# The last down projection as seven block products instead of eight

## The chip, the cores and the metric

The kernel runs on one core of one Trainium2 chip. The metric is device microseconds from start to end of one execution; of a set of runs the median is given. The core's engines, as the profile calls them, are PE (TensorE: matmuls), PEld (its loading of the stationary operand), DVE (VectorE), ACT (ScalarE), POOL (GpSimd) and SP (SyncE, which here only issues DMAs).

## The reference

A decoder trunk of two layers on x of 512 positions by 1024 channels, all in float32. Each layer adds a token mixer (three branches, merged by gates, then `w_out`) and a gated MLP with a causal convolution; a last RMSNorm ends it. The change is in the MLP of the second layer and the norm behind it, and uses idle time in the stages before.

```python
D_MODEL, SEQ, DEPTH, D_FF, CONV_WIDTH = 1024, 512, 2, 2816, 3

def conv_ffn(h, w_up, conv_w, conv_b, w_down):
    S = h.shape[1]
    u = h @ w_up
    up = jnp.pad(u, ((0, 0), (CONV_WIDTH - 1, 0), (0, 0)))
    c = conv_b
    for j in range(CONV_WIDTH):
        c = c + conv_w[j] * up[:, j:j + S]
    gate, val = jnp.split(c, 2, axis=-1)
    return (jax.nn.silu(gate) * val) @ w_down

for l in range(DEPTH):
    ...
    x = x + jnp.sum(gates * proj, axis=2) @ w_out[l]
    x = x + conv_ffn(rmsnorm(x, norm2_g[l]), ffn_w_up[l], ffn_conv_w[l], ffn_conv_b[l], ffn_w_down[l])
return rmsnorm(x, final_g)
```

## The kernel before

All work of the core is written in Python loops that are fully unrolled. A framework then sets the order on each engine: it plays the program through on an estimated timeline, starts on each engine the ready instruction that stands earliest in the program (or was given high priority), hands out buffers as they come free, and adds the semaphores. An engine carries out its instructions in the order so planned. `keep_in_program_order` and `self.pin` fix the order of chosen instructions, here all matmuls of the last stage.

**Matmuls in three parts.** A float32 product is made of three matmuls on parts in the type fp32r: an operand is split into a high part (a cast by ScalarE, L135 for weights) and a low part (a subtraction by VectorE, L136), and `mm3` (matmul at L152) adds high x low, high x high and low x high into one PSUM bank. Every matmul has a stationary operand of 128x128 and a moving one of 128x512.

**Weights.** A unit is 256 KB, 128x512 float32. `unit` asks for the next one; `load` issues its DMA on SP's queue into one of `NRAW` = 3 raw buffers (tile `wr`, L122), `part` splits it. The list of units is known from a first pass, so that loads and splits run ahead of their use, by as many units as `AHEAD` allows for the pool of the unit. The pool says where the parts go: `None` to tiles `wh`, `wl` (three each); "r", "f" and "u" to tiles `sh`, `sl` in those pools; "p" to `wh`, `wl` for three units of five and to `u` tiles for the other two.

**Pools.** 31 tiles `u`, 16 tiles `r` and 39 tiles `f`, each 128x512 float32; PSUM has four banks `acc` and four banks `sm`.

**The stages around the change**, in order: layer 0 ends with `wout` (eight output tiles, 24 matmuls each), `ffn_up` and `ffn_down` (eight output tiles, 66 matmuls each, the result's tile stored to DRAM by POOL's queue). Layer 1 ends with `wout`, `ffn_up` and `last`. `ffn_up` runs over 22 rows of channels i; each has two products of 24 matmuls (gate and value), the scaling (L1054), the convolution (L1056 to L1058), the gate (L1062 to L1064) and the split of the result into `act` (L1066, L1067), two tiles of 128 channels x 512 positions. In layer 1 it also turns x into position-major tiles `xt` by way of DRAM on POOL's queue (L226, L230).

**`last`.** Here the activations are the stationary operand, 128 positions (a chunk c) at a time, and the weights move, so the result has positions on the partitions. It goes through the 1024 output columns in two halves of 512. For each half, for each of the 22 rows k: one unit of weights, four chunks c, three matmuls each. After the first half VectorE adds x piece by piece (L1106), ScalarE squares and sums, POOL multiplies by the norm's weights (L1123). In the second half the last `KEPT` = 6 units stay in `u` tiles, and the four chunks go through them one after another; each chunk's sum, square root (L1137), scaling and store follow at once. The last chunk's store ends the kernel.

Of the kernel before, what the change touches and what calls it, by code (L numbers as in the profile page):

```python
# [8 lines left out]
F32 = mybir.dt.float32  # L9
F32R = mybir.dt.float32r  # L10
# [5 lines left out]
L = 2  # L16
# [8 lines left out]
KEPT = 6  # L25
SEQ = "0 H 0 S 0 U S U S 0 S 0 0 S 2 2 Y 0 0 2 1 2 1 2 1 2 1 2 1 2 1 1 1"
# [22 lines left out]
class Emit:  # L49
# [68 lines left out]
    def load(self, u):  # L118
        name, l, i, c0, n, _ = u
        raw = self.wp.tile([128, 512], F32, name=self.nm("wr"), tag="wr", bufs=NRAW)  # L120
        with self.tc.high_priority():
            self.kept(self.nc.sync.dma_start(raw[:, :n], self.a[name][l, i][:, c0:c0 + n]))  # L122
        self.raws.append(raw)
        self.nraw += 1
# [107 lines left out]

    def norm_new(self):
        return {"z": [], "acc": None}
# [66 lines left out]
    def run(self):  # L301
        nc, tc, a, V = self.nc, self.tc, self.a, self.nc.vector
        self.con = self.cp.tile([128, NCC], F32, name="con")
        self.rst = self.cp.tile([128, 512], F32, name="rst")
# [714 lines left out]
    def wout(self, l, mg, xd, st):  # L1019
        nc, V = self.nc, self.nc.vector  # L1020
        out = []
        for m in range(8):
# [7 lines left out]
            self.norm_sq(st, xi)  # L1030
        return out


    def ffn_up(self, l, st, x):
# [4 lines left out]
        def at():  # L1039
            nt[0] += 1  # L1040
            return (self.f if nt[0] <= NFP else self.r)(dt=F32R, n="ah")
# [3 lines left out]
        for i in range(NFF):  # L1045
# [19 lines left out]
            hi, lo = at(), at()  # L1065
            A.copy(hi, th)  # L1066
            V.tensor_tensor(lo, th, hi, op=SUB)  # L1067
            act.append((hi, lo))
        return act

    def ffn_down(self, l, act, x, st):
# [3 lines left out]
        for m in range(8):  # L1075
# [7 lines left out]
            xd.append(d)  # L1083
        return x, xd


    def last(self, act):


        nc, V, A, P, po = self.nc, self.nc.vector, self.nc.scalar, self.nc.gpsimd, self.tc.keep_in_program_order  # L1090
        fg = [self.u(n="fg") for _ in range(2)]
        for h in range(2):
            nc.sync.dma_start(fg[h], self.a["fgr"][:, 512 * h:512 * h + 512].to_broadcast([128, 512]))
        ss, bias = self.small((128, NC), "fss", 1), self.small((128, NC), "fbi", 1)
        self.pin = True

        def prod(ps, k, c, w):
            cs = slice(128 * c, 128 * c + 128)
            ah, al = act[k]
            self.mm3(ps, (ah[:, cs], al[:, cs]), w, k == 0, k == NFF - 1)  # L1100

        def add(y, ps, j, c):

            b = slice(j % 4 * 128, j % 4 * 128 + 128)
            q = lambda t: t[:, b].rearrange("p (a d) -> p a d", d=32)
            return V.scalar_tensor_tensor(q(y), q(ps), 0.5, self.xt[j][:, c], op0=MUL, op1=ADD)  # L1106

        def square(y, s):
            return A.activation(self.u(n="sq")[:, 0:y.shape[1]], y, AF.Square, accum_out=s)

        self.pool = None
        pss = [self.acc() for _ in range(NC)]
        for k in range(NFF):
            w = self.unit("wdt", 0, k, 0)
            for c in range(NC):
                prod(pss[c], k, c, w)
        ya = []
        for c in range(NC):
            y = self.u(n="ya")
            for j in range(4):  # L1120
                add(y, pss[c], j, c)
            square(y, ss[:, c:c + 1])
            P.tensor_tensor(y, y, fg[0], op=MUL)  # L1123
            ya.append(y)
        V.tensor_scalar(bias, ss, 1.0 / D, 1e-6, op0=MUL, op1=ADD)
        pss = [self.sm() for _ in range(NC)]
        for k in range(NFF - KEPT):
            w = self.unit("wdt", 0, k, 512)
            for c in range(NC):
                prod(pss[c], k, c, w)  # L1130
        self.pool = "u"
        ws = [self.unit("wdt", 0, k, 512) for k in range(NFF - KEPT, NFF)]

# [7 lines left out]
        for c in range(NC - 1):  # L1141
            for k, w in enumerate(ws, NFF - KEPT):
                prod(pss[c], k, c, w)
            y, s = self.u(n="yb"), self.small((128, 1), "fs1")
            for j in range(4, 8):
                po(add(y, pss[c], j, c))
            po(square(y, s))
            rs = factor(s, bias[:, c:c + 1])
            po(A.activation(ya[c], ya[c], AF.Copy, scale=rs))
            nc.scalar.dma_start(self.a["out"][c, :, 0:512], ya[c])  # L1150
            po(V.scalar_tensor_tensor(y, y, rs, fg[1], op0=MUL, op1=MUL))
            nc.sync.dma_start(self.a["out"][c, :, 512:1024], y)
        c, y, b = NC - 1, self.u(n="yb"), bias[:, NC - 1:]
        for k, w in enumerate(ws, NFF - KEPT):
            prod(pss[c], k, c, w)
        for j in range(4, 8):
            po(add(y, pss[c], j, c))
        s = [self.small((128, 1), f"fs{i}", 1) for i in (2, 3)]
        for i in range(2):
            po(square(y[:, 256 * i:256 * i + 256], s[i]))  # L1160
        po(V.scalar_tensor_tensor(b, s[0], 1.0 / D, b, op0=MUL, op1=ADD))
        rs = factor(s[1], b)
        for i in range(2):
            h = slice(256 * i, 256 * i + 256)
            po(V.scalar_tensor_tensor(y[:, h], y[:, h], rs, fg[1][:, h], op0=MUL, op1=MUL))
# [117 lines left out]
```

## Time and profile before

| | |
|---|---|
| time, median of 3 runs | 1713.9 us (1712.93 to 1714.75) |
| span of the profiled execution, first to last instruction | 1712.1 us |
| time of the runs' median around that span | 1.8 us |
| mean granted TensorE clock of the profiled execution | 1.000 |
| `last`: first matmul, end of the last matmul | 1585.80 us, 1705.64 us |
| instructions | 27377 |

The profile is of one execution, and its own time is the span. Times in it are microseconds from its start. A line of the groups has line, engine, operation, output<-inputs, shapes and count, then busy time in all and the mean of one in ns, then the idle time of the engine before it and what ended that. In a timeline a line has start, length, engine, line and operation; what stands in brackets is the idle time before it and the releaser.

### The profile page before, as it was taken

How to read it: one execution, taken by the hardware profiler on the slowest of the kernel's cores; microseconds unless marked ns; L12 is line 12 of the kernel's file. 1: busy time of each engine (PE TensorE's matmuls, PEld its weight loads, DVE VectorE, ACT ScalarE, POOL GpSimd, SP SyncE). 2: the span in 40 equal slices, each digit the busy share in tenths (PEclk: the TensorE clock that was granted, in tenths of full speed). 3: DMA queues.
4: the chain of work that ended last, by engine and by line, in shares of the span. 5: the costliest groups of instructions: out<-in, count | busy, mean ns of one | idle time of the engine just before them, and what ended most of it. 6: DMA issues, size and time to landing. Idle time of an engine off the chain costs nothing.

```text
span 1712.1 us, 27377 instructions
## 1 busy us (share of the span) xinstructions
PE 1701.0 (99%) x10280; PEld 1392.4 (81%) x10280; DVE 1155.0 (67%) x1998; ACT 774.9 (45%) x1315; POOL 178.2 (10%) x213
## 2 busy tenths in 40 slices
PE   9999999999999999999999999999999999999998
PEld 7888777788888888888888888777888888888886
DVE  6887745578669777753368887555776787787333
ACT  6563443554255444433355634345533554444223
POOL 2121000003200000000021210100141011100010
PEclk9999999999999999999999999999999999999999
DMA  5236553525542333233432365535254433333333
GB/s 180 87 109 205 174 174 99 178 89 163 163 148 93 98 99 96 69 113 114 123 105 87 107 222 168 159 122 178 77 185 147 137 122 117 113 109 99 99 99 105
DMA packets 132325, 219.61 MB, mean 128 GB/s; under 512 B 16864, under 2 KB 37088, under 8 KB 132192
## 3 DMA queue, kind: packets, MB, share of 16 engines
q1 hardware_dynamic: 116336, 180.94, 34.4%
q0 software_dynamic: 6784, 20.98, 3.8%
q10 hardware_dynamic: 9072, 15.94, 2.6%
q8 instruction: 81, 1.33, 0.3%
q14 instruction: 52, 0.43, 0.1%
HBM read 188.43 MB, written 29.36 MB: 127 GB/s over the span
## 4 chain that ended last, share of the span: by engine, by line
PE 89%; DMA 5%; DVE 3%; ACT 1%; issue 1%; SPq 1%; ACTq 0%; POOL 0%; DVEq 0%; POOLq 0%
PE acc L152 80%; PE sm L152 4%; PE sm L640 2%; DMA wr<-wall 2%; PE sm L893 1%; DVE wl L136 1%; PE sm L547 1%; DMA ws<-sgw 1%; DMA tr<-yt 0%; DMA tr<-bkT 0%; SPq L226 0%; DMA bkS<-tr 0%; PE sm L998 0%; DMA x<-xT 0%; DMA tr<-qkt 0%
## 5 line engine op out<-in xcount | busy, mean ns | idle before, releaser
L152 PE MATMUL acc<-hi,sh 128*128 128x512 f32 x1108 | 431.9, 390 | 0.0
L152 PE MATMUL acc<-lo,sh 128*128 128x512 f32 x1108 | 431.6, 390 | 0.0
L152 PE MATMUL acc<-hi,sl 128*128 128x512 f32 x1108 | 430.6, 390 | 0.0
L135 ACT CAST sh<-wr 128x512 fp32r<-128x512 f32 (+1 forms) x347 | 212.2, 615 | 356.6 <-PE acc L152 264.3
L136 DVE TENSOR_TENSOR sl<-wr,sh 128x512 fp32r<-128x512 f32 (+1 forms) x347 | 236.1, 683 | 139.9 <-ACT sh L135 74.9
L136 DVE TENSOR_TENSOR wl<-wr,wh 128x512 fp32r<-128x512 f32 x233 | 165.2, 710 | 184.9 <-ACT wh L135 182.3
L135 ACT CAST wh<-wr 128x512 fp32r<-128x512 f32 x233 | 144.1, 619 | 281.1 <-PE acc L152 182.3
L152 PEld LDWEIGHTS acc<-hi,sl 128*128 128x128 f32 x1108 | 208.0, 188 | 43.7 <-DVE gth L1013 0.3
L152 PEld LDWEIGHTS acc<-lo,sh 128*128 128x128 f32 x1108 | 208.0, 188 | 43.6 <-issue 0.9
L152 PEld LDWEIGHTS acc<-hi,sh 128*128 128x128 f32 x1108 | 208.0, 188 | 43.6 <-issue 0.3
L152 PE MATMUL acc<-lo,wh 128*128 128x512 f32 x588 | 232.5, 395 | 0.5 <-DVE lo L211 0.3
L152 PE MATMUL acc<-hi,wl 128*128 128x512 f32 x588 | 230.3, 392 | 0.5 <-DVE wl L136 0.5
L152 PE MATMUL acc<-hi,wh 128*128 128x512 f32 x588 | 229.5, 390 | 0.0
L152 PEld LDWEIGHTS acc<-lo,wh 128*128 128x128 f32 x588 | 110.5, 188 | 26.3 <-DVE lo L211 1.6
L152 PEld LDWEIGHTS acc<-hi,wl 128*128 128x128 f32 x588 | 110.5, 188 | 25.9 <-DVE wl L136 2.3
L152 PEld LDWEIGHTS acc<-hi,wh 128*128 128x128 f32 x588 | 110.6, 188 | 22.4 <-issue 0.2
L152 PE MATMUL acc<-ah,sh 128*128 128x512 f32 x352 | 108.4, 389 | 0.0
L1054 DVE TENSOR_TENSOR fu<-acc,rsF 128x512 f32<-128x512 f32 x88 | 60.6, 688 | 56.4 <-PE acc L152 56.3
L1056 ACT ACTIVATE cv<-fu,pc 128x512 f32<-128x512 f32 x88 | 71.6, 816 | 46.7 <-DVE fu L1054 44.4
L1057 DVE SCALAR_TENSOR_TENSOR cv<-fu,pc,cv 128x511 f32<-128x511 f32 x88 | 65.8, 748 | 21.1 <-ACT cv L1056 20.6
L152 PE MATMUL acc<-wl,hi 128*128 128x512 f32 x192 | 78.3, 408 | 0.0
L152 PEld LDWEIGHTS acc<-ah,sh 128*128 128x128 f32 x352 | 66.1, 188 | 13.7
(312 smaller groups left out, 2345.4 us busy)
## 6 DMA issues: line engine op xcount, KB each, us to landing
wr<-wall SPq DMA_DIRECT2D x488, 256.0 KB, 2.7
gd<-gth ACTq DMA_DIRECT2D x48, 256.0 KB, 3.0
gth<-gd POOLq DMA_DIRECT2D x48, 256.0 KB, 3.6
wr<-wdt SPq DMA_DIRECT2D x44, 256.0 KB, 2.6
wr<-wdn SPq DMA_DIRECT2D x40, 256.0 KB, 2.7
tr<-bkT SPq DMA_DIRECT2D x16, 256.0 KB, 2.8
bkS<-tr SPq DMA_DIRECT2D x128, 32.0 KB, 2.5
tr<-vT SPq DMA_DIRECT2D x8, 256.0 KB, 2.6
```

The lines of the kernel that those rows point to most:

```text
L135: self.kept(self.nc.scalar.copy(hi[:, :n], raw[:, :n]))
L136: self.kept(self.nc.vector.tensor_tensor(lo[:, :n], raw[:, :n], hi[:, :n], op=SUB))
L152: i = self.nc.tensor.matmul(*x, **y)
L547: i = T.matmul(pK[hv[1 - h], j, :], bk[hv[h], c, 1, :], x[hv[h], c, :], start=True, stop=True)
L640: po(T.matmul(o, l, r, start=start, stop=True, skip_group_check=True))
L893: po(T.matmul(X[h][:, i, :], lhsT, rhs, start=new[h], stop=stop, skip_group_check=True))
L1054: V.tensor_tensor(u, ps, self.rsF, op=MUL)
L1056: A.activation(t, u, AF.Identity, scale=self.p("cw2", j), bias=self.p("cb", j))
L1057: V.scalar_tensor_tensor(t[:, 1:], u[:, :511], self.p("cw1", j), t[:, 1:], op0=MUL, op1=ADD)
```

## The change

Rows k are taken in 11 pairs q, positions in two halves of 256, output columns in two halves of 512. With A the activations (positions x channels) in 2x2 blocks and W the weights in 2x2 blocks, the eight block products of `last` become seven, in Winograd's form: seven products of sums of blocks, from which the four output blocks are put together. Each product runs over 11 pairs and two chunks of 128 positions, one unit of weights for each pair.

- **Sums of weights** (`presum`, new): for each pair q, at the end of an output tile's work in `wout` of layer 0 (m = 2, 5), `ffn_down` of layer 0 (m = 0 to 6) and `wout` of layer 1 (m = 2, 5), POOL's queue loads the four blocks into `u` tiles; at the next tile VectorE makes four sums of 128x512 and POOL's queue stores them to DRAM (`tsum`). `last` loads them for four of the seven products and the plain weights for three.
- **Sums of activations** (`halves`, new): in `ffn_up` of layer 1, after each odd row, five VectorE operations of 128x256 make the sums; two of the tiles are split into `act` at once, and two halves `ab` and a half `s4` go to DRAM by POOL's queue. The number of `act` tiles stays the same. `s` and `d` use the tags `wh` and `wl`.
- **`last`** first runs four products side by side (7, 5, 6, 4), over all pairs, in all eight PSUM banks, and meanwhile loads `ab` and `s4` by POOL's queue and splits them into `f` tiles. Then product 1, then 2, then 3, whose last six units stay in `u` tiles and are used by one chunk after the other. VectorE puts the outputs together meanwhile; the second half of the positions is finished and stored during product 2. The weights go to pool "p" instead of `None`. POOL's multiplications are gone.

The diff, cut to its core:

```diff
+PRE = {(0, "o", 2): 0, (0, "o", 5): 1, (0, "d", 0): 2, ..., (0, "d", 6): 8, (1, "o", 2): 9, (1, "o", 5): 10}
     def load(self, u):
+        src = self.tsum[i] if name == "tsum" else self.a[name][l, i]
+    def presum(self, l, stage, m):
+        if self.pre:
+            q, b = self.pre.pop()
+            V.tensor_tensor(b[3], b[3], b[1], op=SUB)
+            V.tensor_tensor(b[1], b[1], b[0], op=SUB)
+            V.tensor_tensor(b[0], b[0], b[3], op=ADD)
+            V.tensor_tensor(b[2], b[2], b[0], op=SUB)
+            for p, t in zip((7, 5, 6, 4), (b[3], b[1], b[0], b[2])):
+                self.tsum[q, p] = self.dp.tile([128, 512], F32, name=self.nm("ts"))
+                self.nc.gpsimd.dma_start(self.tsum[q, p], t)
+        q = PRE.get((l, stage, m))
+        if q is not None:
+            b = [self.u(n="pre") for _ in range(4)]
+            for i, t in enumerate(b):
+                self.nc.gpsimd.dma_start(t, self.a["wdt"][0, 2 * q + i // 2][:, i % 2 * 512:i % 2 * 512 + 512])
+            self.pre.append((q, b))
     def ffn_up(self, l, st, x):
...
-            act.append((hi, lo))
+            if l < L - 1:
+                act.append(self.split(th, at))
+            elif i % 2 == 0:
+                even = th
+            else:
+                act.append(self.halves(even, th, i // 2, at))
+    def halves(self, a, b, q, at):
+        s, d = [self.wp.tile([128, 512], F32, name=self.nm(t), tag=t, bufs=3) for t in ("wh", "wl")]
...
+        P.dma_start(ab[:, h[0]], a[:, h[0]])
+        P.dma_start(ab[:, h[1]], b[:, h[0]])
+        V.tensor_tensor(s[:, h[0]], a[:, h[1]], b[:, h[1]], op=ADD)
+        V.tensor_tensor(s[:, h[1]], s[:, h[0]], a[:, h[0]], op=SUB)
+        V.tensor_tensor(d[:, h[0]], b[:, h[0]], s[:, h[1]], op=SUB)
+        P.dma_start(self.s4[:, h[q % 2]], d[:, h[0]])
+        V.tensor_tensor(b[:, h[0]], a[:, h[0]], a[:, h[1]], op=SUB)
+        return self.split(s, at), self.split(b, at), ab, self.s4
     def last(self, act):
...
+        pss = {p: [(self.acc if p in (7, 5) else self.sm)() for _ in range(2)] for p in (7, 5, 6, 4)}
+        self.pool, ab, s4 = "p", [], []
+        for q in range(Q):
+            s, t = act[q][:2]
+            for p in (7, 5, 6, 4) if q < Q - 1 else (6, 7, 5, 4):
+                w = unit(p, q)
+                x, at = {7: (t, 0), 5: (s, 0), 6: (s, 256), 4: (t, 256)}[p]
+                for r in range(2):
+                    prod(pss[p][r], x, at, r, w, q == 0, q == Q - 1)
...
+            nc.gpsimd.dma_start(o, act[q][2])
+            ab.append(self.split(o, self.f))
...
+        for q in range(3):
+            w = unit(1, q)
+            for r in range(2):
+                go(1, q, r, w)
+        (e: ACT copies of product 6; f, g: combinations of 7, 5, 4 with it, eight in all)
+        for q in range(3, Q):
+            w = unit(1, q)
...
+            if q < 6:
+                for r in range(2):
+                    addx((v1, v2, v3)[q - 3][r], int(q > 3), r + 2 * (q < 5))
+        (product 2, first three pairs; product 1 added to v1, v2, v3 and, with x, to v0;
+         product 2, other pairs, with the norm and the stores of chunks 2 and 3)
+        for q in range(Q - KEPT):
+            w = unit(3, q)
...
+        self.pool = "u"
+        ws = [unit(3, q) for q in range(Q - KEPT, Q)]
+        for r in range(2):
+            for q, w in enumerate(ws, Q - KEPT):
+                go(3, q, r, w)
+            y, ya, b = v3[r], v0[r], ss[:, r:r + 1]
+            po(plus(y, out[3][r], y))
...
```

More of the change, by code (lines that the diff above doesn't have):

```diff
@@ L1102, in add, with unit, prod @@
[L1102 to L1106, printed above, removed]
+        def unit(p, q):
+            if p > 3:
+                return self.unit("tsum", 0, (q, p), 0)
+            return self.unit("wdt", 0, 2 * q + (p > 1), 512 * (p == 3))
+        def prod(ps, x, at, r, w, first, end):
+            cs = slice(at + 128 * r, at + 128 * r + 128)
+            self.mm3(ps, (x[0][:, cs], x[1][:, cs]), w, first, end)
@@ L1139, in factor @@
             return rs
[L1141 to L1152, printed above, removed]
@@ new lines, in last @@
+        out[3] = [self.acc() for _ in range(2)]
+        for q in range(Q - KEPT):
+            w = unit(3, q)
+            for r in range(2):
+                go(3, q, r, w)
+            if q == 1:
+                for r in range(2):
+                    b = ss[:, r:r + 1]
+                    plus(v0[r], out[2][r], v0[r])
+                    square(v0[r], b)
+                    V.tensor_scalar(b, b, 1.0 / D, 1e-6, op0=MUL, op1=ADD)
+                    V.tensor_tensor(v0[r], v0[r], fg[0], op=MUL)
```

157 lines of the change are left out of this document (107 added, 50 removed).

## The prediction

> **What bounds the kernel now.** I read the page first, then the busy time by stage, then the engines' timelines inside the last stage.
>
> ```profile
> span 1712.1 us, 27377 instructions
> PE 1701.0 (99%) x10280; PEld 1392.4 (81%) x10280; DVE 1155.0 (67%) x1998; ACT 774.9 (45%) x1315; POOL 178.2 (10%) x213
> PE 89%; DMA 5%; DVE 3%; ACT 1%; issue 1%; SPq 1%; ACTq 0%; POOL 0%; DVEq 0%; POOLq 0%
> ```
>
> TensorE is busy 99% of the span and carries 89% of the chain that ended last. The stage view (core 0; columns: length, busy and count of PE, PEld, DVE, ACT, POOL, clock, DMA share, GB/s) says the same of each stage that the change touches: ffn_down of layer 0, ffn_up of layer 1, and `last`.
>
> ```profile
> 700.00:800.00 100.00, 100.00 (x443) 82.81 (x442) 54.14 (x88) 36.10 (x61) 1.62 (x3) 1.00 0.33 97
> 1400.00:1500.00 100.00, 100.00 (x443) 82.78 (x442) 78.44 (x121) 45.72 (x72) 10.93 (x20) 1.00 0.37 114
> 1580.00:1645.00 65.00, 65.00 (x288) 53.64 (x287) 23.44 (x38) 17.57 (x28) 0.00 (x0) 1.00 0.31 101
> 1645.00:1679.00 34.00, 34.00 (x152) 28.15 (x151) 13.42 (x27) 10.47 (x21) 5.95 (x4) 1.00 0.33 100
> ```
>
> In `last` nothing but matmuls counts: PE never idles and VectorE is a third busy. What a matmul costs there is not its printed duration. The timeline of PE at the start of `last` and at its end:
>
> ```profile
> 1585.80 0.39 PE L152 MATMUL acc<-wl,ah 128*128 128x512 f32 x1
> 1586.48 0.39 PE L152 MATMUL acc<-wl,ah 128*128 128x512 f32 x1
> 1587.16 0.39 PE L152 MATMUL acc<-wl,ah 128*128 128x512 f32 x1
> 1705.03 0.61 PE L152 MATMUL sm<-sh,ah 128*128 128x512 f32 x2
> ```
>
> Each line opens a triple of three matmuls. Triples start 0.68 us apart, so a matmul takes 0.2267 us although each is shown as 0.39: they overlap. The stage has 22 rows x 2 halves x 4 chunks x 3 = 528 matmuls; 528 x 0.2267 = 119.7 us, and from 1585.80 to the end at 1705.64 it is 119.84. The tail after it is 6.5 us.
>
> **What the change removes.** Seven products x 11 pairs x 2 chunks x 3 = 462 matmuls: 66 fewer, 66 x 0.2267 = 15.0 us. (At the printed 0.39 us it would be 25.7; the pitch decides.) If PE stayed full, `last` would take 104.7 us.
>
> **What it asks in return: weights.** Before, one weight unit (256 KB load, cast by ScalarE, subtraction by VectorE) serves 12 matmuls, 2.72 us. Now a unit serves 6, 1.36 us, and there are 77 units instead of 44. No steady stage of before asks for more than one unit in 2.72 us, so the rate must come from a burst. There is one: near the end the last loads go to tiles that are free, and nothing but the three raw buffers (`NRAW`) holds them back. ScalarE's casts, then some of VectorE's subtractions, then SyncE's issues:
>
> ```profile
> 1679.72 0.62 ACT L135 CAST sh<-wr 128x512 fp32r<-128x512 f32 x1 [0.62 <-DMA wr<-wdt]
> 1681.20 0.62 ACT L135 CAST wh<-wr 128x512 fp32r<-128x512 f32 x1 [0.86 <-PE sm L152]
> 1682.50 0.62 ACT L135 CAST sh<-wr 128x512 fp32r<-128x512 f32 x1 [0.68 <-DMA wr<-wdt]
> 1684.08 0.62 ACT L135 CAST sh<-wr 128x512 fp32r<-128x512 f32 x1 [0.95 <-DMA wr<-wdt]
> 1685.43 0.62 ACT L135 CAST sh<-wr 128x512 fp32r<-128x512 f32 x1 [0.74 <-DMA wr<-wdt]
> 1686.94 0.62 ACT L135 CAST sh<-wr 128x512 fp32r<-128x512 f32 x1 [0.88 <-DMA wr<-wdt]
> 1688.41 0.62 ACT L135 CAST sh<-wr 128x512 fp32r<-128x512 f32 x1 [0.85 <-DMA wr<-wdt]
> ...
> 1680.37 0.69 DVE L136 TENSOR_TENSOR sl<-wr,sh 128x512 fp32r<-128x512 f32 x1 [0.55 <-ACT sh L135]
> 1684.73 0.69 DVE L136 TENSOR_TENSOR sl<-wr,sh 128x512 fp32r<-128x512 f32 x1 [0.88 <-ACT sh L135]
> ...
> 1681.09 0.33 SPq L122 DMA_DIRECT2D wr<-wdt  x1
> 1685.45 0.33 SPq L122 DMA_DIRECT2D wr<-wdt  x1
> ```
>
> Six intervals from 1679.72 to 1688.41 give 1.45 us a unit. One buffer's round: its subtraction ends at 1680.37 + 0.69 = 1681.06, SyncE issues at 1681.09, the next weights land and are cast at 1684.08 (3.02 us after the release), the subtraction ends at 1684.73 + 0.69 = 1685.42, and SyncE issues again at 1685.45. The round is 4.36 us; three buffers give 1.45 us. That is more than the 1.36 that PE now asks for, with VectorE and ScalarE otherwise idle and no other transfers. So in the new stage the supply of weights, not PE, ends last.
>
> **What is in stock at the start.** While ffn_up ends, weights of `last` are loaded ahead:
>
> ```profile
> 1583.36 0.33 SPq L122 DMA_DIRECT2D wr<-wdt  x1
> 1590.22 0.33 SPq L122 DMA_DIRECT2D wr<-wdt  x1
> 1580.84 0.69 DVE L136 TENSOR_TENSOR wl<-wr,wh 128x512 fp32r<-128x512 f32 x1 [0.18 <-ACT wh L135]
> ```
>
> By 1583.4 six loads were out, three split and three waiting for a `wh` tile; SyncE then stood until PE gave one back. In the new stage every five units take three `wh`/`wl` tiles and two `u` pairs, so five units can be split and three more landed when PE starts. Unit 5 is split once unit 0 is used (1.36 + 0.65 + 0.69 = 2.7 us), its buffer loads unit 8, which is ready 3.0 + 1.34 later, at 7.0 us; PE wants it at 8 x 1.36 = 10.9. With c the us per unit, the 77th unit is ready at 7.0 + 68c, and after it PE still has 3 + 18 matmuls (the six kept units go through chunk 0, then chunk 1): 4.8 us. So the stage takes 11.8 + 68c, never less than 104.7. Against 119.7 the gain is 107.9 - 68c: 9.3 us at c = 1.45, 5.2 at 1.51, nothing at 1.587, and the full 15.0 only below 1.367.
>
> **What raises c.** Other transfers: 11 `ab` and 6 `s4` loads of 256 KB on POOL's queue during the first 44 units. Landing (last column, us) beside such loads in the merges, in a stretch with more traffic (175 GB/s), in the present `last` and in its burst:
>
> ```profile
> wr<-wall SPq DMA_DIRECT2D x49, 256.0 KB, 2.8
> gth<-gd POOLq DMA_DIRECT2D x22, 256.0 KB, 3.6
> ...
> wr<-wall SPq DMA_DIRECT2D x37, 256.0 KB, 3.2
> ...
> wr<-wdt SPq DMA_DIRECT2D x27, 256.0 KB, 2.6
> ...
> wr<-wdt SPq DMA_DIRECT2D x5, 256.0 KB, 2.9
> ```
>
> The new stage moves 256 KB per 1.45 us, 181 GB/s, plus about 40 for `ab` and `s4`. From the burst's 2.9 to 3.2 is +0.3 on a round, +0.1 on c, at most for the loads that meet another; I take +0.03. The Trainium skill, DMA: Bandwidth & Descriptors, section Latency and other measured facts, puts HBM access at 0.2 us on average and 2 us under high load; that speaks against any change that nearly doubles a stage's loads. If the whole 1.8 us came on top, c would be (4.36 + 1.8)/3 = 2.05, an estimate from that page; the rows above show tenths so far.
>
> VectorE and ScalarE: behind each unit's split stand the new operations. Prices by the nearest rows (mean ns of one after the comma):
>
> ```profile
> L1054 DVE TENSOR_TENSOR fu<-acc,rsF 128x512 f32<-128x512 f32 x3 | 2.1, 687 | 1.2 <-PE acc L152 1.2
> L1106 DVE SCALAR_TENSOR_TENSOR ya<-acc,xt 128x128 f32<-128x128 f32 x16 | 3.4, 280 | 2.1 <-PE acc L152 2.1
> 1644.61 2.26 DVE L1106 SCALAR_TENSOR_TENSOR ya<-acc,xt 128x128 f32<-128x128 f32 x11
> L1165 DVE SCALAR_TENSOR_TENSOR yb<-yb,frs,fg 128x256 f32<-128x256 f32 x2 | 0.9, 481 | 0.0
> L1151 DVE SCALAR_TENSOR_TENSOR yb<-yb,frs,fg 128x512 f32<-128x512 f32 x3 | 2.3, 752 | 0.1
> L1137 ACT ACT_TABLE_LOAD x1 | 1.3, 1283 | 0.0
> ```
>
> In the first 44 units: one more split per four units and half of one. A split of 0.6 us fits into the 1.45 us round behind the unit's own; half of them collide for some 0.3 us: +0.04 on c. In products 1 and 2 (22 units, 32 us at 1.45) VectorE has 22 x 0.65 = 14 us of splits, 14 combinations of a full tile x 0.69 = 9.7, 32 pieces of 128x128 at 2.26/11 = 0.205 = 6.6, and four scalings x 0.75 = 3: 33 us. It is full, so a split often finds an operation in front of it: half of 0.69 at every second round, +0.06 to +0.1, and part spills into the last product, which has little else. The square root's table load (1.3 us) moves here from the first chunk of the end, beside a stock of nothing; once. Together c = 1.51. Bounds: the round with the shortest landing of the burst, released at 1679.82 and cast at 1682.50, is 2.68 + 1.34 = 4.02, c = 1.34 (full gain); one 0.69 us operation ahead of every split gives (4.36 + 0.69)/3 = 1.68 (6.3 us lost).
>
> **The rest.** Sums of weights: 11 steps x 4 VectorE operations x 0.69 us = 30 us, and 88 transfers of 256 KB on POOL's queue. ffn_down of layer 0, where seven of the steps lie, has VectorE 54% busy and PE at 100% beside it; free. In w_out a step's 2 MB meet weights that PE wants one per 2.72 us, with three raw buffers and three split units in hand (8 us): I take 0.5 us in all, 0 to 3. What queues behind these on POOL is the store of x for the next layer, long before its use. ffn_up of layer 1: five half-width operations per pair, by the row above 0.48 each, 2.4 us in the 96 matmuls x 0.2267 = 21.8 of a pair; VectorE's 78% becomes 89%; PE has four accumulators, and covers it. Without that cover it would be 2.4 us once, at the last pair. Three stores per pair on POOL: hidden. Tail: one full-tile operation instead of four quarter ones (0.69 against 0.89): 0.2 won; otherwise the same.
>
> Sum: 107.9 - 68 x 1.51 = 5.2, + 0.2, - 0.5 = 4.9 won. The profiled span would be 1707.2. The runs' median of 1713.9 lies 1.8 above the span, so 1709.0.
>
> **Rivals.** (a) *VectorE takes the gain*: with every split behind one whole operation, products 1 and 2 and the `ab` splits alike, c = 1.68 and the stage is 6.3 us longer: 1720.2 less the tail's 0.2, plus 0.5: 1720.5. It decides from 1.587 on, that is 0.4 us of added wait in a round of 4.36. For it: 33 us of work in 32. Against: splits are given high priority when the order is planned, and the other operations have until the next product. (b) *PE stays the bound*: c below 1.367, 15 us won: 1698.9. Only the shortest landing speaks for it. (c) *Landings grow with load*: by the longest landing seen for such a load, about 1.1 us over the burst's (4.0 against 2.9), as in the answer on the weight buffer:
>
> ```profile
> DMA to landing us min/median/max: 2.4/2.6/4.0
> ```
>
> c = (4.36 + 1.1)/3 = 1.82 and 15.9 us lost: 1730. (The Trainium skill's rule named above would be worse still.) Against: it is the longest, and the median is 2.6. (d) *The two cancel*: c from 1.54 to 1.63, within 3.4 us of now.
>
> **How the numbers follow.** 0.2% is 3.4 us, about what a measurement of this kernel can tell from no change. Forecast, c from 1.43 to 1.54: 0.50, its own range 1703 to 1711. (a) 0.24, (b) 0.10, (c) 0.06, (d) 0.10. Faster: the forecast less its edge, and (b): 0.55. Same: (d) and the edge: 0.15. Slower: (a), (c): 0.30. The range leaves out (c), the outer part of (a) and half of (b): 1699 to 1723.
>
> **What would show it.** In the changed profile: 66 fewer matmuls; in `last` PE idle for the first time, some 8 to 11 us in many gaps of tenths of a us, released by `wl`/`sl` of L136's kind; casts of `wr` released by the DMA, not by PE; casts 1.45 to 1.55 us apart in the first four products and wider in products 1 and 2; PE still 100% in ffn_up and ffn_down. I am wrong if PE is full in `last` (b), if the casts stand 1.6 us or more apart (a, c), or if PE waits in w_out or ffn_up.

## The result, and the profile after

| | before | after |
|---|---|---|
| time, median | 1714.1 us (4 runs) | 1754.4 us (4 runs, 1752.5 to 1757.7) |
| ratio | | 1.0238, interval 1.0224 to 1.0253 |
| span of the profiled execution | 1712.1 us | 1752.1 us |
| `last`: first matmul | 1585.80 us | 1609.86 us |
| `last`: first matmul to end of the last | 119.84 us | 135.27 us |
| after the last matmul | 6.46 us | 6.97 us |

The forecast was 1709.0 us, the range 1699 to 1723. The kernel became 40 us slower: 24.1 us lie ahead of `last`, 15.4 in it, 0.5 behind it. The page of the kernel after:

```profile
span 1752.1 us, 27897 instructions
PE 1714.1 (98%) x10214; PEld 1384.6 (79%) x10214; DVE 1237.7 (71%) x2161; ACT 799.4 (46%) x1365; POOL 249.9 (14%) x353
PE 79%; DMA 10%; DVE 6%; ACT 2%; issue 2%; SPq 1%; POOL 0%; ACTq 0%; DVEq 0%; POOLq 0%
```

PE has the 66 matmuls less (10214 against 10280), and is yet busy 13.1 us longer. It also idles, 38 us in all (11 before): in the chain that ended last PE fell from 89% to 79%, DMA and VectorE doubled. Slices of 5 us show where (columns as in the stage view of the prediction):

```profile
505.00:510.00 5.00, 2.40 (x11) 1.67 (x9) 0.00 (x0) 0.00 (x0) 0.00 (x0) 1.00 0.95 346
510.00:515.00 5.00, 4.00 (x12) 3.13 (x12) 3.96 (x7) 2.27 (x4) 0.42 (x1) 0.66 0.22 74
1365.00:1370.00 5.00, 2.53 (x12) 1.76 (x10) 0.30 (x1) 0.00 (x0) 0.00 (x0) 1.00 0.81 309
1620.00:1625.00 5.00, 3.09 (x13) 2.17 (x12) 1.18 (x3) 1.01 (x2) 1.92 (x4) 1.00 0.97 311
1625.00:1630.00 5.00, 3.31 (x9) 2.17 (x10) 1.32 (x2) 1.24 (x2) 1.07 (x2) 0.66 1.04 388
1685.00:1690.00 5.00, 1.48 (x4) 1.19 (x5) 4.67 (x9) 3.91 (x8) 0.00 (x0) 0.80 0.56 173
1720.00:1725.00 5.00, 1.99 (x5) 1.60 (x6) 4.95 (x13) 2.19 (x6) 0.18 (x1) 0.71 0.52 146
```

Two kinds of stall. In `wout` of layer 0 and layer 1 (505, 1365) and at the start of `last` (1620, 1625) the DMA engines are busy at 0.81 to 1.04 and VectorE and ScalarE all but stand still. Later in `last` (1685, 1720) DMA is half idle and VectorE is full: there its order decides. In the slice of the stall or in the one behind it the clock column falls to 0.66 to 0.80.

The second sign stands in the timeline of PE at the start of `last`:

```profile
1609.86 0.39 PE L155 MATMUL acc<-wl,ah 128*128 128x512 f32 x1
1610.56 0.40 PE L155 MATMUL acc<-wl,ah 128*128 128x512 f32 x1
1611.26 0.39 PE L155 MATMUL acc<-wl,ah 128*128 128x512 f32 x1
```

PE waits for nothing here, but the triples start 0.70 us apart, not 0.68: 0.2333 us a matmul in place of 0.2267. That is most of why fewer matmuls keep PE busy longer: with the pitch of 0.68 back (the second kernel below) PE is busy 1702.3 us, 11.8 less. This is still 1.3 us more than before with 66 matmuls less, and the mean granted clock of that run is 0.991, not 1.000.

### The profile page after: what moved, and what is told of

It is laid out like the page before. It is cut to its first block, busy times and chain, and to the rows that moved or that the text cites. A ratio compares the mean times of both kernels' runs of the same rounds, so it can differ in the third digit from the quotient of the medians.

```text
span 1752.1 us, 27897 instructions
## 1 busy us (share of the span) xinstructions
PE 1714.1 (98%) x10214; PEld 1384.6 (79%) x10214; DVE 1237.7 (71%) x2161; ACT 799.4 (46%) x1365; POOL 249.9 (14%) x353
## 4 chain that ended last, share of the span: by engine, by line
PE 79%; DMA 10%; DVE 6%; ACT 2%; issue 2%; SPq 1%; POOL 0%; ACTq 0%; DVEq 0%; POOLq 0%
PE acc L155 73%; DMA wr<-ts 2%; PE sm L663 2%; DMA wr<-wall 2%; DMA wr<-wdt 2%; DVE wl L139 1%; DVE sl L139 1%; DMA xi<-xT 1%; PE sm L916 1%; ACT sh L138 1%; PE sm L570 1%; ACT wh L138 1%; SPq L229 1%; DMA tr<-qkt 1%; DMA ws<-sgw 1%
## 5 line engine op out<-in xcount | busy, mean ns | idle before, releaser
L138 ACT CAST sh<-wr 128x512 fp32r<-128x512 f32 (+1 forms) x375 | 228.7, 615 | 374.3 <-PE acc L155 218.9
L139 DVE TENSOR_TENSOR sl<-wr,sh 128x512 fp32r<-128x512 f32 (+1 forms) x375 | 254.5, 682 | 132.8 <-ACT sh L138 99.4
L155 PE MATMUL acc<-wl,hi 128*128 128x512 f32 x212 | 87.0, 410 | 0.0
L155 PE MATMUL acc<-wh,lo 128*128 128x512 f32 x212 | 83.4, 394 | 0.0
L155 PE MATMUL acc<-wh,hi 128*128 128x512 f32 x212 | 83.4, 394 | 0.0
```

Source lines behind the costliest of these rows:

```text
L138: self.kept(self.nc.scalar.copy(hi[:, :n], raw[:, :n]))
L139: self.kept(self.nc.vector.tensor_tensor(lo[:, :n], raw[:, :n], hi[:, :n], op=SUB))
L155: i = self.nc.tensor.matmul(*x, **y)
```

## The experiments

Times are medians, each beside the kernel before on the same chip: 1714.0 us for the first four kernels, 1715.7 for the next four, then 1716.2, 1716.1 and 1715.0. These differ by some 2 us, so a time is best read against the kernel before beside it.

### The pitch of a matmul

The change dropped the small tile `fbi`, 32 bytes for each partition, which was laid out ahead of the `f` tiles. So every `f` tile starts at 1312 instead of 1344 modulo 2048, no longer at a multiple of 64 bytes. One line gives the 32 bytes to the kernel before, where they shift its `f` tiles away (to 1376), and to the kernel after, where they bring them back to 1344:

```diff
+        V.memset(self.small((128, NC), "gap", 1), 0.0)
```

On the kernel before:

> The kernel before with one more small tile of 32 bytes per partition, so that every tile of the f pool starts 32 bytes later (no longer at a multiple of 64 bytes); nothing else moves. Theory A (the address of the moving operand sets the pitch of a matmul: 233.3 ns in the changed kernel's merges, w_out and ffn_down against 226.6 before, where f tiles are the moving operand): some 1,700 matmuls with f tiles as moving operand become 6.7 ns slower, the kernel 9 to 12 us longer (1723 to 1726), the triple pitch in ffn_down 0.70 us instead of 0.68. Theory B (the slower pitch comes from the added transfers or VectorE's sums): no change, 1714, pitch 0.68.

Measured: 1727.7 us, ratio 1.0078 (1.0063 to 1.0093), so 13.7 us lost by 32 bytes, 1.7 more than the theory allowed. One thing more moved: the tiles of the mixer's own pool, which begins where the `f` pool begins. In layer 0 that cost about 1 us at most: the first load behind the mixer (`gup`) starts at 303.9 us instead of 302.9. `last` of this kernel, else unchanged, has the slow pitch:

```profile
1597.60 0.39 PE L152 MATMUL acc<-wl,ah 128*128 128x512 f32 x1
1598.30 0.40 PE L152 MATMUL acc<-wl,ah 128*128 128x512 f32 x1
```

On the kernel after:

> The changed kernel with one more small tile of 32 bytes per partition, so that its f tiles start where they do in the kernel before. Theory A: 9 to 12 us less than the changed kernel, 1743 to 1746, pitch in ffn_down 0.68 us although the sums and their transfers are all there. Theory B: no change, 1754, pitch 0.70.

Measured: 1744.6 us, 9.8 less than after, pitch 0.68 again:

```profile
1602.11 0.39 PE L155 MATMUL acc<-wl,ah 128*128 128x512 f32 x1
1602.79 0.39 PE L155 MATMUL acc<-wl,ah 128*128 128x512 f32 x1
```

The address is shown, in both directions. All that follows stands on this second kernel where it concerns `last`; it is called the shifted kernel from here on.

### The sums of weights

The kernel before, with the sums made and stored, and its own `last`:

```diff
+    def presum(self, l, stage, m):   # and its calls in wout and ffn_down
```

> The kernel before, with the sums of weights made and stored as in the changed kernel, but never used: the last projection is the old one. f tiles lie as before. Theory (the sums cost time where they are made in w_out: loads in bursts of four on POOL's queue make the loads of x late, VectorE waits for them in order, PE runs dry and its clock falls): 1724 to 1730, with PE below full and the clock below 1 in both w_out stages and nowhere else. Rival (the sums are hidden, as predicted, and all of the loss is the last stage's and the addresses'): 1714 to 1716.

Measured: 1728.7 us, ratio 1.0085 (1.007 to 1.010): the sums cost 14.8 us, and the other 15.9 to the shifted kernel come with its new `last`. In `ffn_down`, first to last eviction, nothing changed (102.9 us before and here); the loss lies in the two `wout`. The rows of POOL, SP and VectorE there, and the landings in this stretch (last column, us):

```profile
499.13 2.13 POOL L251 DMA_DIRECT2D pre<-wdt  x4
499.91 0.44 SPq L1046 DMA_DIRECT2D xi<-xT  x1
500.97 0.69 DVE L138 TENSOR_TENSOR sl<-wr,sh 128x512 fp32r<-128x512 f32 x1
507.73 0.69 DVE L1049 SCALAR_TENSOR_TENSOR xi<-acc,xi 128x512 f32<-128x512 f32 x1 [6.07 <-DMA xi<-xT]
509.87 0.68 DVE L138 TENSOR_TENSOR sl<-wr,sh 128x512 fp32r<-128x512 f32 x1
...
pre<-wdt POOLq DMA_DIRECT2D x4, 256.0 KB, 6.9
xi<-xT SPq DMA_DIRECT2D x3, 256.0 KB, 7.2
```

POOL issues the four loads of a step within 2.13 us, on top of the last step's stores; SP's load of x for the next output tile goes out among them, at 499.91, and lands 7.8 us later, at 507.7. VectorE's next operation in order is the one that adds this x. It also empties a PSUM accumulator. It waits 6.07 us, and the weight splits wait behind it, from 500.97 to 509.87. PE has four accumulators `acc`; when the next output tile needs the one that this operation has not emptied, PE stops. It starts again at 508.47, right behind the operation's end (507.73 + 0.69 = 508.42), and 1.4 us before the next weight split starts. The waits of PE in the two `wout` (total, times, longest):

```profile
PE acc L154 <- DVE xi L1049: 4.5, 2, 4.2
PE acc L154 <- DVE xi L1049: 3.9, 1, 3.9
```

So the late x reaches PE by way of the accumulator, not of the weights. To tell whether the transfers, the operations or this wait count, three kernels:

```diff
-            V.tensor_tensor(b[3], b[3], b[1], op=SUB)   # and the other three
```

> e3 without VectorE's four operations: the blocks are loaded and stored as before, but no sums are made (nobody uses them). Theory (transfers make x late in w_out): still 1724 to 1729, VectorE waits for the x load as in e3. Rival (the sums in VectorE's queue stand before the eviction and the splits): 1714 to 1718.

Measured: 1718.3 us, ratio 1.0013 (1.0004 to 1.0022): 2.6 us, so the theory, that the transfers alone do it, missed. Without the operations POOL's stores need not wait for VectorE, so the loads of a step also go out earlier; it is not a pure removal.

```diff
-                self.nc.gpsimd.dma_start(self.tsum[q, p], t)
-                self.nc.gpsimd.dma_start(t, self.a["wdt"]...)
+                self.nc.gpsimd.memset(t, 0.0)
```

> The kernel before, with VectorE's four sums of each of the 11 steps on tiles that GpSimd sets to zero, and without the loads and stores of the weight sums (their result is unused, and the old last stage stands). Transfers alone cost 2.6 us, both together 14.8. Theory (an operation that waits for its data holds up the weight splits behind it on VectorE): without loads to wait for they cost little, 1714 to 1718. Rival (VectorE's 30 us themselves are in the way in w_out and ffn_down): 1722 to 1728.

Measured: 1718.4 us, ratio 1.0015 (1.0005 to 1.0024): 2.2 us. So 2.6 and 2.2 apart, 14.8 together: neither the transfers alone nor VectorE's 30 us alone are the cost. In both runs PE waits for the same operation, 2.5 and 2.2 us in all. Then the wait itself, with all transfers and operations in place:

```diff
-            xi = self.u(n="xi")
-            nc.sync.dma_start(xi, xd[m])
+            while len(xs) < min(m + 3, 8):
+                xs.append(self.u(n="xi"))
+                nc.sync.dma_start(xs[-1], xd[len(xs) - 1])
+            xi = xs[m]
```

> The kernel before with the sums of weights made and stored and the old last stage (1728.7, 14.8 above the kernel before), and the loads of x in w_out issued two output tiles earlier. Theory (VectorE waits up to 6 us for an x load that lands late behind the four loads and stores of a step, and the weight splits stand behind that wait): most of what w_out loses comes back, 8.8 us in layer 0 and 9.6 in layer 1 less some given back later: 1717 to 1721. Rival (the weights themselves are late): 1726 to 1730.

and the control, the same edit in the kernel before:

> The kernel before, with the loads of x in w_out issued two output tiles earlier: the control for the run with the sums. VectorE waits there at most 1 us for x, and PE hardly: 1712 to 1715 by every theory. If it wins or loses more than 2 us, the comparison with the sums is to be taken against this kernel.

Measured: 1715.9 us with the sums, 1716.1 in the control, both with ratio 0.9998 (0.9989 to 1.0007 and 0.9988 to 1.0007). With x loaded two tiles earlier the sums cost nothing that can be measured, a little better than expected. The stretch that stood still, in the run with sums:

```profile
505.00:510.00 5.00, 5.00 (x24) 4.14 (x23) 2.35 (x4) 2.88 (x4) 0.00 (x0) 1.00 0.50 164
1365.00:1370.00 5.00, 5.00 (x24) 4.14 (x23) 4.96 (x9) 4.25 (x6) 0.00 (x0) 1.00 0.41 119
```

PE is full in both, and in the whole run it never waits for the operation that adds x. That settles it: a late load of x, needed by the operation that frees PE's accumulator. VectorE waited for x in the kernel before too, longer than the expectation of the control has it:

```profile
DVE xi L1027 <- DMA xi<-xT: 5.0, 3, 3.1
```

5.0 us in three places, 3.1 at most. PE's four accumulators covered that: PE has no wait for this operation in that run, and so the early x alone brings nothing.

One try to move the cost away went otherwise, all steps put into `ffn_down` of layer 0 of the shifted kernel:

```diff
+PRE = {(0, "d", 0): (0, 1), (0, "d", 1): (2, 3), (0, "d", 2): (4, 5), (0, "d", 3): (6, 7), (0, "d", 4): (8,), ...}
```

> e2 with the four sums that were made in the two w_out stages moved to ffn_down of layer 0 (there two pairs of rows at each of the first four output tiles, one at the next three). Theory (bursts of POOL's loads and stores in w_out make x late): PE full in both w_out stages, 12 to 15 us less than e2, 1730 to 1733; ffn_down may lose up to 2 us. Rival (any step of sums costs the same wherever it is made): as e2, 1742 to 1747.

A miss: 1741.3 us, 25.5 above its kernel before, where the shifted kernel is 30.7 above its own. From first to last eviction `wout` of layer 0 was as long as in the kernel before (29.3 us against 29.5), but `ffn_down` went from 102.9 to 110.9. Two steps for each tile are too dense there also.

### The last stage

A table of `last` in the shifted kernel and its variants: first matmul to the copies of product 6 (the first four products), and from there to the last eviction, which follows the last matmul at once. The variants:

```diff
-NU, NR, NFP = 31, 16, 39
-NRAW = 3
+NU, NR, NFP = 30, 16, 39
+NRAW = 4
```

> The changed kernel with aligned f tiles as in e2, four raw weight buffers instead of three and 30 u tiles instead of 31. Theory (the last stage is bound by the round of three raw buffers, 4.4 us and more): the round is shared by four, c falls from the 1.81 us a unit measured to about 1.36, PE is nearly full again except at the burst of loads at the start and the change to product 1; the last stage falls from 135 to 108 to 118 us, the kernel to 1717 to 1728. Rival (VectorE and ScalarE in their order hold the splits, or the transfers' own speed): the stage stays within 4 us of e2's, 1740 to 1746.

```diff
-            o = self.u(n="ab")          # the loads of ab and s4 and their splits
-            nc.gpsimd.dma_start(o, act[q][2])
-            ab.append(self.split(o, self.f))
...
-            x, at = {1: (ab[q], 0), 2: (ab[q], 256), 3: (s4[q // 2], q % 2 * 256)}[p]
+            x, at = {1: (act[Q - 1][0], 0), 2: (act[Q - 1][0], 256), 3: (act[Q - 1][1], q % 2 * 256)}[p]
```

> The changed kernel with its tiles shifted back by 32 bytes, and the 17 loads of ab and s4 and their splits left out of the last stage: products 1 to 3 use tiles of the last pair in their place (that is the part of the computation left out). Theory (the burst of GpSimd's queue and the splits behind it made c 1.81 where 1.51 was forecast): the last stage falls from the 136 us of the shifted kernel to 11.8 + 68 x 1.48, some 112, plus about 5 for the change of products, 117 in all; the time falls from 1744.6 to 1720 to 1728. Rival (the doubled rate of weights limits itself, or VectorE's combinations do): at most 6 us won, 1738 to 1744.

with four buffers also:

> As the kernel without feature loads, with four raw buffers for weights instead of three (one tile u less). It leaves out the same part. Theory (three buffers are the limit of supply once the burst is gone): c falls below the 1.36 us that PE asks, PE is nearly full, the stage takes 105 to 111 us and the time is 1712 to 1720. Rival (VectorE's order in products 1 and 2 or the memory limits it): within 3 us of the kernel with three.

```diff
-            A.activation(e, pss[6][r], AF.Copy, scale=0.5)   # and all plus and addx of products 1 and 2,
-                square(ya, b)                                # the norm of chunks 2 and 3
+                P.memset(t[r], 0.0)
```

> The changed kernel shifted back by 32 bytes (1744.6), without the combinations of the products and the norm of the third and fourth chunk on VectorE and ScalarE in products 1 and 2 and the first part of product 3 (that part of the computation is left out; the stores of the output stay, from tiles set to zero). The loads of ab and s4 stay. In the shifted kernel the first four products take 78.8 us, product 1 and the front of 2 take 19.5, the next stretch 21.4; at 1.45 us a unit the last two would be 32 together. Theory (VectorE's order holds the weight splits there): 8 to 12 us won, 1733 to 1738, all of it behind the first four products. Rival (these products are slow through the supply itself): under 3 us won.

and both of the last two edits:

> As the kernel without combinations, and without the loads of ab and s4 and their splits too (products 1 to 3 use tiles of the last pair). The sum of the prediction without its disturbances: the stage takes 11.8 + 68 x 1.43 to 1.45 = 109 to 110.5 us against 126.8 without the loads alone; the time is 1736.9 less some 16, 1719 to 1723. Rival (PE's clock or a third cost in the stage): 1726 to 1732.

| kernel | time, us | first four, us | rest, us | `last`, us |
|---|---|---|---|---|
| shifted | 1744.6 | 78.8 | 57.7 | 136.5 |
| four raw buffers | 1733.4 | 73.1 | 54.0 | 127.1 |
| no loads of `ab`, `s4` | 1736.9 | 64.6 | 62.5 | 127.1 |
| the same, four buffers | 1726.2 | 61.1 | 53.4 | 114.5 |
| no combinations | 1738.8 | | | 125.7 |
| neither | 1733.3 | | | 120.2 |

The stretches of the shifted kernel (up to the copies, to product 1's first use, to product 2's, to the end), then those without the loads:

```profile
1602.10:1680.90 78.80, 66.03 (x265) 48.92 (x263) 44.98 (x71) 38.13 (x66) 10.69 (x20) 0.98 0.68 208
1680.90:1700.40 19.50, 18.82 (x71) 15.28 (x72) 13.21 (x31) 7.55 (x14) 0.00 (x0) 0.84 0.50 154
1700.40:1721.80 21.40, 15.94 (x61) 12.13 (x60) 19.41 (x49) 10.55 (x22) 2.17 (x4) 0.84 0.52 165
1721.80:1738.60 16.80, 16.23 (x69) 12.43 (x68) 8.90 (x18) 7.13 (x15) 0.00 (x0) 1.00 0.37 118
```

```profile
1602.20:1666.80 64.60, 62.44 (x264) 49.80 (x263) 33.11 (x52) 27.72 (x46) 2.16 (x4) 0.97 0.58 176
1666.80:1687.30 20.50, 17.99 (x74) 12.78 (x73) 17.85 (x46) 8.29 (x15) 0.00 (x0) 1.00 0.48 153
1687.30:1710.60 23.30, 17.45 (x61) 13.18 (x60) 14.84 (x33) 11.01 (x23) 2.17 (x4) 0.85 0.54 177
1710.60:1729.30 18.70, 16.83 (x69) 12.27 (x67) 10.75 (x19) 8.42 (x17) 0.00 (x0) 1.00 0.37 111
```

The loads cost the first stretch 14.2 us (78.8 to 64.6, where 264 matmuls at 0.2267 need 59.8), but 4.8 us of that is lost again in the rest: 9.4 in the stage. In the third stretch VectorE is busy 19.41 of 21.40 us; with the combinations gone the stage is 10.8 us shorter (some 9 of them behind its first 264 matmuls), and 6.9 shorter where the loads are gone already (that run has a burden of its own, below). Four buffers won 11.2 us in time, 9.4 in the stage, less than expected. The expectations for the run without loads (1720 to 1728) and with four buffers (1712 to 1720) missed by 9 and 6 us; the first had the change of products at 5 us. That for the run without combinations (1733 to 1738) missed by 1.

How the loads act, in the kernel after: POOL's issues, ScalarE's casts, and the landings from 1608 to 1632:

```profile
1618.21 0.54 POOL L1161 DMA_DIRECT2D ab<-ab  x1
1618.73 0.54 POOL L1166 DMA_DIRECT2D s<-s  x1
1619.26 1.06 POOL L1161 DMA_DIRECT2D ab<-ab  x2
...
1624.28 0.62 ACT L138 CAST sh<-wr 128x512 fp32r<-128x512 f32 x1 [3.89 <-DMA wr<-ts]
1627.49 0.62 ACT L138 CAST wh<-wr 128x512 fp32r<-128x512 f32 x1 [2.59 <-DMA wr<-ts]
...
wr<-ts SPq DMA_DIRECT2D x10, 256.0 KB, 4.0
ab<-ab POOLq DMA_DIRECT2D x6, 256.0 KB, 7.4
fg<-fgr POOLq DMA_DIRECT2D x2, 256.0 KB, 6.5
```

The `u` tiles are free at that time, so nothing spaces the loads, and the weights land after 4.0 us instead of 2.6. Once the burst is over, 28 intervals of casts from 1636.89 to 1680.15 give 1.545 us a unit.

With neither loads nor combinations 1719 to 1723 was expected; 1733.3 is past the rival's range too. The stage is still 120.2 us:

```profile
1604.00:1630.00 26.00, 22.92 (x91) 17.52 (x90) 14.95 (x26) 11.06 (x18) 8.08 (x16) 0.93 0.63 194
1630.00:1715.00 85.00, 81.98 (x349) 63.87 (x348) 39.85 (x59) 35.32 (x57) 0.00 (x0) 1.00 0.62 181
1715.00:1724.20 9.20, 7.82 (x27) 5.69 (x25) 3.01 (x6) 4.26 (x7) 0.00 (x0) 0.81 0.03 11
...
1627.17 0.62 ACT L138 CAST wh<-wr 128x512 fp32r<-128x512 f32 x1 [1.69 <-DMA wr<-ts]
1716.25 0.62 ACT L138 CAST sh<-wr 128x512 fp32r<-128x512 f32 x1 [0.28 <-DMA wr<-wdt]
```

From the 16th unit's cast to the 77th's are 61 intervals in 89.08 us, 1.46 a unit: three raw buffers give what the burst of before gave. With that, 11.8 + 68 x 1.46 is 111.1, and 9.1 us are unaccounted for. The 77th unit is ready at 1716.25 + 1.34, 113.6 us after the start and not 106.3: the stock was late by 7.3 us, in the first 26 us, where the two broadcast loads `fg` (landing 6.4 us) and the end of `ffn_up` lie. The other 1.8 are PE's last matmuls at a clock of 0.81. That the `fg` loads are the cause of the late start was not tried alone. Nor is this the bare stage: with the combinations gone, nothing holds back the four 256 KB stores of the output that stay. POOL issued them from 1611.27 to 1617.41, around the `fg` loads. The first 264 matmuls took some 67.6 us here, and 64.4 in the run that left out the loads alone and has no such stores there. Without these 3.2 us the bare stage would be some 117 us, an estimate from the two runs, 3 less than the 119.84 of before; and the combinations are worth some 10 us here too, as where the loads stand.

### Spacing the loads

Three kernels spaced the `ab` and `s4` loads by fewer tiles; all three missed.

```diff
-            o = self.u(n="ab")
+            o = self.wp.tile([128, 512], F32, name=self.nm("ab"), tag="ab", bufs=1)
```

> e4 with the loads of ab and s4 in the last stage through one tile of their own instead of any free u tile (29 u tiles left), so that a load starts only when the last one has been split. Theory (ten loads of POOL in 9 us stretch the landing of the weights to 6.5 us and starve PE): the 6 to 9 us at the start of the stage go, 1724 to 1728; landings of weights there stay below 4 us. Rival (the weights are late because the order of splits holds them): no change, 1731 to 1735.

Measured: 1763.2 us. One tile makes a round of some 5 us for each load and split; the copies of product 6 stand in ScalarE's order behind the last of these casts, and PE waits for them once for 24.4 us.

The same, with all sums in `ffn_down` and the copies of product 6 ahead in the plan:

```diff
-            A.activation(e, pss[6][r], AF.Copy, scale=0.5)
+            with self.tc.high_priority():
+                A.activation(e, pss[6][r], AF.Copy, scale=0.5)
```

> e6 with the sums of e5 and with high priority for the two copies of product 6 that product 1 waits for. Sum of the parts: 1733.4 - 13 (sums) - 7 (spacing) - 3 (copies) = 1710, range 1704 to 1716. If the parts are not independent (the same stalls counted twice) it stays at 1716 to 1722.

Measured: 1749.4 us; high priority for the copies did not help, PE waited 25.6 us for them.

Three tiles, the copies ahead, and 27 tiles `u` to make room:

```diff
-NU, NR, NFP = 30, 16, 39
+NU, NR, NFP = 27, 16, 39
+            o = self.wp.tile([128, 512], F32, name=self.nm("ab"), tag="ab", bufs=3)
```

> The changed kernel shifted back by 32 bytes, four raw buffers, the loads of ab and s4 through three tiles of their own (so at most three are under way), 27 tiles u, and ScalarE's copies of product 6 ordered with high priority. Theory (the burst costs its landings and the copies stand too late): 1733.4 with four buffers falls to 1723 to 1729. Rival (what costs is the splits behind these loads, not their burst): 1731 to 1736, or more where the splits get late.

Measured: 1748.7 us. The first four products took 64.7 us (1619.00 to 1683.74) instead of 73.1, as the theory has it; but three tiles less in `u` made the stages ahead slower, and `last` began 20.7 us later than with 30 tiles.

### All causes mended

The shifted kernel with both edits from above:

```diff
+NRAW = 4
+                nc.sync.dma_start(xs[-1], xd[len(xs) - 1])
```

> The changed kernel shifted back by 32 bytes, with four raw buffers (1733.4) and the loads of x in w_out two output tiles earlier. It computes all of the reference. Theory (the causes add: the early x takes the 12 to 13 us of the sums back, and the last stage stays at 126.9 us): 1718 to 1723, 4 to 9 above the kernel before. Rival (with the sums gone from the path, the last stage meets less stock and loses more): 1725 to 1732.

Measured: 1721.7 us (1717.6 to 1729.9), ratio 1.0038 (1.0024 to 1.0053), as the sum of the parts had it. `last` begins at 1586.7 and takes 126.9 us.

```diff
-            o = self.u(n="ab")
+            o = (self.f if q < 8 else self.u)(n="ab")
-                V.tensor_tensor(b, b, self.xt[4 * h + j][:, c], op=ADD)
+                P.tensor_tensor(b, b, self.xt[4 * h + j][:, c], op=ADD)
-            if q < 5:     # norm of chunks 2 and 3, in product 2
+            if q > 2:     # the same block, in product 3
```

> As the kernel with four raw buffers and early x, and three edits more: the first loads of ab and s4 go to f tiles, which come free pair by pair, so that they are spaced by PE; the additions of x to the combinations go from VectorE to GpSimd; the norm of the third and fourth chunk moves from product 2 to the end of the plain part of product 3. It computes all of the reference. Theory (the burst and VectorE's order are what is left): spacing brings 6 to 8 us of the 9.6 back and the lighter VectorE 3 to 6 of the 10.7: 1706 to 1714, at or below the kernel before. Rival (GpSimd's operations and the later splits take it back): 1716 to 1724.

Measured: 1718.6 us, ratio 1.0019 (1.0010 to 1.0028): the rival's range. Its two parts of `last`, and those of the kernel above:

```profile
1586.90:1659.00 72.10, 62.97 (x266) 48.65 (x264) 45.38 (x74) 38.28 (x69) 11.25 (x21) 1.00 0.73 232
1659.00:1710.20 51.20, 48.62 (x198) 39.25 (x198) 35.85 (x67) 23.48 (x47) 16.51 (x28) 0.93 0.51 164
...
1586.70:1660.40 73.70, 63.46 (x266) 48.47 (x264) 45.40 (x74) 38.38 (x69) 10.68 (x20) 1.00 0.69 225
1660.40:1713.60 53.20, 49.73 (x198) 40.10 (x198) 39.15 (x92) 23.63 (x47) 2.18 (x4) 0.91 0.46 150
```

The first part, where the loads are spaced, is 1.6 us shorter, not 6 to 8; the second, where VectorE does less, 2.0. The spacing did take place: in the first 40 us the `ab` loads land after 3.8 us instead of 7.3 (medians), but the weights after 4.2 instead of 4.5. So what the loads cost seems to be less their burst than themselves, 17 loads and 17 splits more in the same order. With three tiles of their own, and the copies ahead, the first four products had won 8.4 us (the stage 5.0), and what tells the two ways of spacing apart stays open. No version beat the kernel before.

## Why the prediction was wrong

Of the 40.5 us between 1754.4 (after) and 1714.0 (the kernel before beside the first four kernels), 9.8 are the address, 14.8 the sums and 15.9 come with the new `last`. By the steps of the prediction:

- **66 matmuls less, and the pitch decides**: held, but the pitch was taken as a constant of the operation. It was 0.2333 us in the kernel after, in `last` and wherever an `f` tile is an operand. Nothing in the trace of before showed this; no step or rival had it.
- **Supply of weights, not PE, ends last**: held. With neither loads nor combinations c was 1.46 from the 16th unit on, where the burst of before gave 1.45.
- **c = 1.51 with everything added**: this is the term of the stage that failed. 135.3 = 11.8 + 68c gives 1.82. All that was added to 1.45 came to 0.06, some 4 us over 68 units. The `ab` and `s4` loads, +0.07 in 44 units (3 us), cost 9.4; the combinations, +0.06 to +0.1 in 22 units (some 2 us), cost 10.8. Both were priced as an average over the rounds. The loads came in a burst, but spacing them brought back only 1.6 us, so why they cost 9.4 stays open in part; the combinations cost theirs where VectorE was full. Rival (a) had the second mechanism and rival (c) the first; each alone was too small. That (c)'s c is 1.82 too is chance.
- **Stock at the start**: it was said to be ready at 7.0 us for the ninth unit; with neither loads nor combinations the supply still ran 7.3 us late, of which some 3 go with the early stores of that run.
- **Sums in w_out, 0.5 us, 0 to 3**: the largest single error, 14.8. The step counted the weights that PE has in hand and never asked what else the loads delay. x came late in the kernel before already (5.0 us in three places). VectorE waits for it in order, and PE waits for the accumulator that VectorE then frees (8.4 us in the two `wout`, and a lower clock behind).
- **ffn_down free, ffn_up free**: held for the seven steps that the change put into `ffn_down`, not for eleven; `ffn_up` of layer 1 lost little (PE waits 1.3 us once at its start).
- **What would show it**: casts at 1.6 us or more, or PE waiting in w_out, was named as wrong; both came, the casts only in part. In the kernel after they stood 2.26 us apart on average in the burst (1612.03 to 1636.89), then 1.545 as forecast, then 1.77 (1680.15 to 1738.56).

On landings, the Trainium skill, DMA: Bandwidth & Descriptors, Latency and other measured facts, has 0.2 us for an access to HBM on average and 2 us at high load. Here the weights' landing went from 2.6 us to 4.0 at 311 to 388 GB/s, so the rule that the prediction set aside agrees in sign, and in size to 0.4 us, for the start of the stage. Whether the memory or the DMA engines, busy at 0.97 and 1.04 there, made the landings long is not shown.

## What to carry over

Where an engine works in order, ask of every new burst of transfers which load it delays, and what the operation that waits for that load holds up, accumulators included: here two cheap parts cost 14.8 us together and nothing once that load was issued earlier. A stage at the limit of its supply has no room to average over: check what the stage wins with the bare work before adding the rest. Here that is some 3 us by the estimate above, less than either addition costs. And compare the addresses of the operands before the traces: 32 bytes cost 10 to 14 us.

## What the hardware showed unexpectedly

**Address.** With the `f` tile that they read at a multiple of 64 bytes matmuls take 0.2267 us each, shifted by 32 bytes 0.2333, whether that tile is the moving operand (merges, `wout`, `ffn_down`) or holds the stationary one (`last`). Three addresses were run, modulo 2048: 1344, and 1312 and 1376, both 32 bytes off.

**Clock after a stall.** A stall costs more than its idle time. In the run without combinations, behind a wait of 3.17 us:

```profile
1621.47 0.79 PE L155 MATMUL sm<-wl,ah 128*128 128x512 f32 x1 [3.17 <-DVE wl L139]
1622.91 0.63 PE L155 MATMUL sm<-wl,ah 128*128 128x512 f32 x1
1624.19 0.51 PE L155 MATMUL sm<-wl,ah 128*128 128x512 f32 x1
1625.00 0.39 PE L155 MATMUL sm<-wl,ah 128*128 128x512 f32 x1
```

Triples 1.44, 1.28 and 0.81 us apart, then 0.68 again: 1.5 us lost over the wait. The Trainium skill, TensorE: Matmul & The Clock Gate, Part 1, has a half clock after an idle window of some 3.4 us, until some 3.4 us of work. These rows agree in the pace (about twice the pitch for the first 2.7 us); the wait was a little shorter than that window.
